# Five waits in the order model of a hybrid layer's mixing stage, set anew

## The chip, the cores and the metric

One Trainium2 chip, one core of it. The metric is the device time of one launch in microseconds (us). Times of the kernel before: 1146.1 us, the median of three runs (1145.75 to 1147.96).

## The reference

One layer on 512 tokens of width 1024, in float32: a SwiGLU half step (inner width 2816), a mixing step with two branches side by side, a second SwiGLU half step, a final norm. The mixing step is where the change is:

```python
h = rms_norm(x, mix_norm[l]); proj = h @ w_in[l]
p_rwkv, p_att, p_gate = jnp.split(proj, [RWKV_COLS, RWKV_COLS + ATT_COLS], axis=-1)
y_rwkv = rwkv7_branch(p_rwkv, ...)      # delta-rule recurrence over the tokens, 8 heads of 64
y_att = attention_branch(p_att, ...)    # window of 128, 8 query heads, 2 key heads, sinks
gate_rwkv, gate_att = jnp.split(jax.nn.sigmoid(p_gate), 2, axis=-1)
merged = gate_rwkv * (y_rwkv @ w_branch_rwkv[l]) + gate_att * (y_att @ w_branch_attn[l])
x = x + merged @ w_out[l]
```

## The kernel before, in words

Activations lie transposed, channels on the partitions and the 512 tokens along the free axis. Every large product is made of three matmuls (`mm3`, lines 216 to 218) of a rounded high half and a low half of each operand. ScalarE rounds a weight tile to its high half (line 196), VectorE subtracts it to get the low half (line 197), so each weight tile costs VectorE one pass.

The mixing stage computes 34 **jobs**, one per 128 columns of `w_in`: a job is 24 matmuls of 128 by 512. A job's result is evacuated by VectorE or, for the 16 gate jobs `g0` to `g15`, copied by ScalarE (`gt`, line 700), multiplied on GpSimd (line 701) and written to DRAM (`gd`, line 702). Later it is loaded again (line 1307 for the attention half, line 1329 for the other) and goes through a sigmoid on ScalarE (lines 1308 and 1330).

Beside this **dense** stream run five **lanes**, written as Python generators:

- `prep(i)`, one per pair of heads (i = 0 to 3), turns the columns `k`, `r`, `v` into chunked operands: `AR`, `BK` (VectorE, lines 868 to 883), then the Gram matrices `GT` (16 rows of small matmuls in two halves, line 895 on; their PSUM banks are emptied by VectorE on line 899), transposes of `BK`, and `UV`. Sums over heads go through `head_sums` (lines 802 to 813): VectorE makes a low half (line 807), then two matmuls with `bones` (lines 810 and 811).
- `solve(i)` inverts the triangular blocks on VectorE (lines 941 and 943) with DMA round trips, and ends with a load of `GI` (line 1003).
- `wkv(i)` is the recurrence: VectorE transposes `GI` into `YT` (lines 1016 and 1017), then come short rounds of small matmuls, each followed by copies on ScalarE and VectorE (lines 1027, 1037, 1038, 1057, 1058, 1069 to 1071, 1088 to 1104), six steps from chunk to chunk (line 1109), the output, and a norm through `head_sums`. `wkv(2)` and `wkv(3)` are the last ones.
- `att_kv` and `att(i)`: scores, softmax (`S`, lines 1223 to 1245), transposes of `S`, the product with the values.

When all lanes have ended come the products with `w_branch_attn` (96 matmuls on the operands `yas`) and `w_branch_rwkv` (96 matmuls on `xh`, `xl` again, whose operands are the split results of the `wkv` lanes, line 222), then `w_out`.

**What sets the order.** `interleave` (line 100) runs the generators once, before anything runs on the chip. `pe.clock` is a running sum of modelled TensorE time. A lane that yields a wait w over 300 is resumed when the clock has advanced by 1.15 w + 200 (`SLACK`, ns); one that yields less, by w. While no lane is ready, dense quarters of six matmuls (1390 ns each) are issued; a share of them is also issued beside lane work (`RATIO`, `LUMP`). So a wait decides only how much dense work stands between a lane's step and its next one in the engines' queues. The tile framework then schedules the instructions that the program gives it, and adds the semaphores. Each engine takes its queue in order. PSUM banks for small products come from two rings of three banks, "a" and "b" (`pssm`); a new product on a ring waits until the bank from three products before has been emptied.

```python
yield WSUM                                 # head_sums, line 808: 13 uses
yield 1000.0                               # prep, line 884: after AR's second half
yield 0.0                                  # prep, line 901: after GT's evictions
yield 1800.0                               # wkv, line 1018: after the transposes of GI
yield 1600.0                               # att, line 1246: after S is scaled
```

Of the kernel before, what the change touches and what calls it, by code (L numbers as in the profile page):

```python
# [50 lines left out]
LATE = 6  # L51
GEV = 1
AHEAD = 2
WSUM = 1200.0
HOP = 900.0
SLACK = 1.15, 200.0

# [74 lines left out]
def hybrid_layer_kernel(  # L132
# [47 lines left out]
    def pssm(st="a"):  # L180
        return ps.tile([P, T], F32, tag="sm" + st, name="sm", bufs=3)
# [620 lines left out]
    def head_sums(x_, sx="a"):  # L802
# [4 lines left out]
        v.tensor_tensor(out=lo, in0=x_, in1=hi.bitcast(F32), op=ALU.subtract)  # L807
        yield WSUM
        o = pssm(sx)
# [17 lines left out]
    def prep(i):  # L827
# [53 lines left out]
        yield 1200.0  # L881

        v.tensor_tensor(out=AR[:, :, 1, :], in0=c3(rm), in1=c3(E2), op=ALU.mult)
        yield 1000.0


        while i > 1 and i - 2 not in ended:
# [2 lines left out]
        for n2 in range(0, NCH // 2, 2):  # L890
            pg = [pssm().rearrange("p (n a c) -> p n a c", n=2, c=C) for h in (0, 1)]
            with sp.together():
                for n in (n2, n2 + 1):
                    for m in (0, 1):
                        for h in (1, 0):
                            sp.matmul(pg[h][:, n - n2, m:4:2, :], lhsT=BK[HS[h], 2 * n + m, :, :],
                                      rhs=AR[HS[h], 2 * n + m, :, :], start=True, stop=True)
            for h in (0, 1):
                v.tensor_tensor(out=GT[:, n2:n2 + 2, h, 0:4, :], in0=pg[h],
                                in1=gmask.unsqueeze(1).broadcast_to([P, 2, 4, C]), op=ALU.mult)  # L900
            yield 0.0
        for n2 in range(0, NCH // 2, 2):
            pt_ = pssm()
            for j in range(4):
# [102 lines left out]
    def wkv(i, sx):  # L1007
# [7 lines left out]
        YTv = YT.rearrange("p (n c) -> p n c", c=32)  # L1015
        v.transpose(YTv[0:32], GI[0:32, :, 0:32])
        v.transpose(YTv[64:96], GI[64:96, :, 0:32])
        yield 1800.0
        p1 = pssm(sx)
        with sp.together():  # L1020
            for n in range(NCH):
# [183 lines left out]
    def att(i):  # L1205
# [37 lines left out]
        v.reciprocal(out=dn, in_=dn)  # L1243
        yield 5000.0
        v.tensor_tensor(out=S, in0=S, in1=dn.unsqueeze(3).broadcast_to([P, 2, NB, P]), op=ALU.mult)
        yield 1600.0

        Pc = slot("Pc2", (P, 2, T))
        Pp = S.rearrange("p h b c -> p h (b c)")
# [30 lines left out]
    def lane_p(j):  # L1280
        for i in (j, j + 2):
            while i > 1 and st[i - 1] is None:
                yield 300.0
            yield from prep(i)
            yield from solve(i, st[i])

    def lane_w(j):
        for i in (j, j + 2):
            yield from wkv(i, "ab"[j])

    def lane_a():
        yield from att_kv()
        for i in range(4):
            yield from att(i)
        yield 3000.0
        load_yas()
        yield 3000.0
# [165 lines left out]
```

## Time and profile before

| | |
|---|---|
| median of 3 runs | 1146.1 us |
| the profiled execution | 1146.73 us |
| its span in the profile | 1145.0 us |
| granted TensorE clock, mean over the span | 0.994 |
| TensorE matmul busy | 1110.8 us, 97% |
| VectorE busy | 867.9 us, 76% |
| ScalarE busy | 588.8 us, 51% |
| GpSimd busy | 224.4 us, 20% |

The mixing stage lies at 395 to 717 us of the span. The profile's matmul ends are modelled and matmuls overlap, so the start-to-start distance of matmuls, not their length, tells TensorE's pace. Engine names in rows: PE is TensorE, PEld its weight loads, DVE VectorE, ACT ScalarE, POOL GpSimd, SP the queue of DMA issues (SPq). "[0.95 <-DVE GT L899]" behind a row means that the engine had been idle for 0.95 us and that a VectorE instruction of line 899 released it.

### The profile page before, as it was taken

The numbers are of one execution on the slowest core, as the hardware profiler recorded it, in microseconds if no ns is written. First come the engines' busy times: TensorE is split into PE (matmuls) and PEld (weight loads), VectorE is DVE, ScalarE is ACT, GpSimd is POOL, SyncE is SP. The second block draws the span as 40 slices with busy tenths as digits, with TensorE's granted clock in tenths as the row PEclk, the third lists the DMA queues.
The fourth block names the chain that finished last, engine by engine and source line by source line (L and its number), as shares of the span: only waits on it lengthen the run. The fifth ranks groups of instructions, "written<-read, shape, count | busy, mean of one in ns | idle before, by whom it ended". The sixth has DMA issues, their size and how long they took to land.

```text
span 1145.0 us, 19776 instructions
## 1 busy us (share of the span) xinstructions
PE 1110.8 (97%) x7892; PEld 963.3 (84%) x7892; DVE 867.9 (76%) x1149; ACT 588.8 (51%) x943; POOL 224.4 (20%) x164
## 2 busy tenths in 40 slices
PE   9899999999999999899989999999999999999997
PEld 7699899978997687678767877778999899989985
DVE  6978579955988479999697635778996489945865
ACT  5744145523555665557553656467554155523554
POOL 5022024402301000000111220012431034202200
PEclk9999999999999999999999999999999999999999
DMA  9234323432226453434325634933334233432221
GB/s 269 64 92 130 92 76 109 129 94 74 70 74 184 138 182 72 107 100 121 91 82 142 167 105 147 268 118 100 95 111 129 74 93 109 132 96 71 75 92 74
DMA packets 223068, 130.12 MB, mean 114 GB/s; under 512 B 37727, under 2 KB 204448, under 8 KB 222976
## 3 DMA queue, kind: packets, MB, share of 16 engines
q1 hardware_dynamic: 221248, 126.79, 38.4%
q10 hardware_dynamic: 1184, 2.04, 0.6%
q8 instruction: 62, 1.02, 0.4%
q0 software_dynamic: 544, 0.04, 0.1%
q14 instruction: 30, 0.25, 0.1%
HBM read 112.96 MB, written 15.61 MB: 112 GB/s over the span
## 4 chain that ended last, share of the span: by engine, by line
PE 72%; DVE 16%; DMA 4%; ACT 4%; issue 2%; SPq 1%; POOL 0%; ACTq 0%; DVEq 0%
PE sm L441 32%; PE mm L216 9%; PE mm L217 8%; PE mm L218 8%; PE sm L218 3%; PE sm L216 3%; PE sm L217 3%; DVE wl L197 3%; PE sm L90 3%; DVE pr L941 2%; DMA g<-gd 1%; ACT wh L196 1%; DMA wr<-in_ffn_w_gate_dram 1%; DVE xt L400 1%; DVE W L943 1%
## 5 line engine op out<-in xcount | busy, mean ns | idle before, releaser
L197 DVE TENSOR_TENSOR wl<-wr,wh 128x1024 fp32r<-128x1024 f32 (+2 forms) x149 | 208.3, 1398 | 80.8 <-ACT wh L196 80.1
L196 ACT CAST wh<-wr 128x1024 fp32r<-128x1024 f32 (+2 forms) x149 | 147.6, 990 | 219.2 <-PE mm L217 99.5
L429 POOL TENSOR_TENSOR wx<-wr,wx 128x1024 f32<-128x1024 f32 x40 | 115.2, 2881 | 386.2 <-DVE wl L197 249.8
L441 PE MATMUL sm<-th,wh 128*128 128x256 f32 x640 | 181.0, 283 | 0.9 <-DVE xt L429 0.9
L197 DVE TENSOR_TENSOR wl<-wx,wh 128x1024 fp32r<-128x1024 f32 x100 | 160.3, 1609 | 27.4 <-ACT wh L196 26.6
L441 PE MATMUL sm<-tl,wh 128*128 128x256 f32 x640 | 180.2, 282 | 0.0
L441 PE MATMUL sm<-th,wl 128*128 128x256 f32 x640 | 180.1, 281 | 0.0
L196 ACT CAST wh<-wx 128x1024 fp32r<-128x1024 f32 x100 | 104.9, 1049 | 132.2 <-PE sm L441 79.7
L441 PE MATMUL sm<-xh,wl 128*128 128x256 f32 x480 | 135.9, 283 | 0.6 <-DVE wl L197 0.6
L441 PE MATMUL sm<-xh,wh 128*128 128x256 f32 x480 | 136.0, 283 | 0.0
L441 PE MATMUL sm<-xl,wh 128*128 128x256 f32 x480 | 135.7, 283 | 0.0
L216 PE MATMUL mm<-xh,wh 128*128 128x512 f32 x320 | 131.1, 410 | 1.2 <-ACT wh L196 0.9
L218 PE MATMUL mm<-xh,wl 128*128 128x512 f32 x320 | 127.6, 399 | 3.2 <-DVE wl L197 2.9
L217 PE MATMUL mm<-xl,wh 128*128 128x512 f32 x320 | 126.5, 395 | 0.0
L441 PEld LDWEIGHTS sm<-th,wh 128*128 128x128 f32 x640 | 120.7, 189 | 2.1 <-issue 1.4
L441 PEld LDWEIGHTS sm<-tl,wh 128*128 128x128 f32 x640 | 120.6, 189 | 0.0
L441 PEld LDWEIGHTS sm<-th,wl 128*128 128x128 f32 x640 | 120.4, 188 | 0.0
L441 PEld LDWEIGHTS sm<-xh,wl 128*128 128x128 f32 x480 | 91.7, 191 | 0.8 <-DVE wl L197 0.8
L441 PEld LDWEIGHTS sm<-xh,wh 128*128 128x128 f32 x480 | 91.7, 191 | 0.5 <-ACT acc L1346 0.2
L441 PEld LDWEIGHTS sm<-xl,wh 128*128 128x128 f32 x480 | 91.7, 191 | 0.5 <-issue 0.2
L218 PEld LDWEIGHTS mm<-xh,wl 128*128 128x128 f32 x320 | 60.5, 189 | 18.4 <-DVE wl L197 3.8
L216 PEld LDWEIGHTS mm<-xh,wh 128*128 128x128 f32 x320 | 60.5, 189 | 16.1 <-issue 2.0
(391 smaller groups left out, 2259.4 us busy)
## 6 DMA issues: line engine op xcount, KB each, us to landing
wr<-in_ffn_w_down_dram SPq DMA_DIRECT2D x38, 512.0 KB, 4.1
wr<-in_w_in_dram SPq DMA_DIRECT2D x34, 512.0 KB, 4.2
wr<-in_ffn_w_gate_dram SPq DMA_DIRECT2D x42, 256.0 KB, 3.0
wr<-in_ffn_w_up_dram SPq DMA_DIRECT2D x42, 256.0 KB, 3.4
wx<-in_ffn_w_gate_dram SPq DMA_DIRECT2D x40, 256.0 KB, 3.0
wx<-in_ffn_w_up_dram SPq DMA_DIRECT2D x40, 256.0 KB, 3.5
gd<-gt SPq DMA_DIRECT2D x16, 256.0 KB, 2.3
g<-gd SPq DMA_DIRECT2D x16, 256.0 KB, 3.3
```

The lines of the kernel that those rows point to most:

```text
L90: self.keep(self.pe.matmul(out, lhsT=lhsT, rhs=rhs, **k))
L196: s.copy(out=hi[:, c], in_=raw[:, c])
L197: v.tensor_tensor(out=lo[:, c], in0=raw[:, c], in1=hi[:, c].bitcast(F32), op=ALU.subtract)
L216: pe.matmul(acc, lhsT=ah, rhs=bh, start=(first and k == 0), stop=False)
L217: pe.matmul(acc, lhsT=ah, rhs=bl, start=False, stop=False)
L218: pe.matmul(acc, lhsT=al, rhs=bh, start=False, stop=(last and k == n - 1))
L400: v.scalar_tensor_tensor(out=t_[:, 1 + i, :], in0=b0, scalar=g1, in1=b1, op0=ALU.mult, op1=ALU.add if i == 2 else ALU.subtract)
L429: e.tensor_tensor(out=o, in0=a, in1=b, op=op)
L441: pe.matmul(acc, lhsT=x_, rhs=y_, start=first and j == 0 and k == 0 and i == 0, stop=last and k == n - 1 and i == 2, skip_group_check=True)
L941: v.tensor_tensor(out=pv_[:, m], in0=a_[:, m].unsqueeze(2).broadcast_to(sh), in1=b_[:, m].rearrange("p u c -> p c u").unsqueeze(1).broadca ...
L943: v.tensor_reduce(out=o, in_=pv_, axis=AX.X, op=ALU.add)
```

## The change

Five waits of the order model get larger numbers. No instruction of the program is added or taken away, and no operand changes.

```diff
-WSUM = 1200.0
+WSUM = 1800.0
...
         v.tensor_tensor(out=AR[:, :, 1, :], in0=c3(rm), in1=c3(E2), op=ALU.mult)
-        yield 1000.0
+        yield 2400.0
...
                 v.tensor_tensor(out=GT[:, n2:n2 + 2, h, 0:4, :], in0=pg[h],
                                 in1=gmask.unsqueeze(1).broadcast_to([P, 2, 4, C]), op=ALU.mult)
-            yield 0.0
+            yield 1400.0
...
         v.transpose(YTv[64:96], GI[64:96, :, 0:32])
-        yield 1800.0
+        yield 2900.0
...
         v.tensor_tensor(out=S, in0=S, in1=dn.unsqueeze(3).broadcast_to([P, 2, NB, P]), op=ALU.mult)
-        yield 1600.0
+        yield 2800.0
```

What it moves is seen in the order of the instructions on each engine. Three places follow, each before and after. In them `mm<-xh,wh`, `mm<-xl,wh` and `mm<-xh,wl` are dense matmuls, `sm` is a small product's bank.

**First place**, TensorE, the Gram matrices of the first pair, `prep(0)`. Before:

```order
L90 MATMUL sm<-AR,BK 128x2x64 x9
L217 MATMUL mm<-xl_148,wh 128x512
L218 MATMUL mm<-xh_140,wl 128x512
L216 MATMUL mm<-xh_141,wh 128x512
L217 MATMUL mm<-xl_149,wh 128x512
L218 MATMUL mm<-xh_141,wl 128x512
L216 MATMUL mm<-xh_142,wh 128x512
L217 MATMUL mm<-xl_150,wh 128x512
L218 MATMUL mm<-xh_142,wl 128x512
L90 MATMUL sm<-AR,BK 128x2x64 x7
L96 MATMUL sm<-ident,BK 128x128 x4
```

Now, at the same place:

```order
L90 MATMUL sm<-AR,BK 128x2x64 x8
L810 MATMUL sm<-hi,bones 128x512
L811 MATMUL sm<-lo,bones 128x512
L216 MATMUL mm<-xh_141,wh 128x512
L217 MATMUL mm<-xl_149,wh 128x512
L218 MATMUL mm<-xh_141,wl 128x512
L216 MATMUL mm<-xh_142,wh 128x512
L217 MATMUL mm<-xl_150,wh 128x512
L218 MATMUL mm<-xh_142,wl 128x512
L90 MATMUL sm<-AR,BK 128x2x64 x8
```

The head sum of the other lane now stands between the two halves, and takes a bank of the same ring "a"; the transposes of `BK` have moved twelve dense matmuls further back.

**Second place**, TensorE, the start of the last recurrence, `wkv(3)`. Before:

```order
L218 MATMUL mm<-xh_142,wl 128x512
L90 MATMUL sm<-YT,GT 32x32 x16
L216 MATMUL mm<-xh_143,wh 128x512
L217 MATMUL mm<-xl_151,wh 128x512
L218 MATMUL mm<-xh_143,wl 128x512
L216 MATMUL mm<-xh_144,wh 128x512
L217 MATMUL mm<-xl_152,wh 128x512
L218 MATMUL mm<-xh_144,wl 128x512
L90 MATMUL sm<-GI,YT 32x32 x16
```

Now:

```order
L218 MATMUL mm<-xh_146,wl 128x512
L90 MATMUL sm<-YT,GT 32x32 x16
L216 MATMUL mm<-yas,wh 128x512
L217 MATMUL mm<-yas,wh 128x512
L218 MATMUL mm<-yas,wl 128x512
L216 MATMUL mm<-yas,wh 128x512
L217 MATMUL mm<-yas,wh 128x512
L90 MATMUL sm<-GI,YT 32x32 x16
```

Before, 84 dense matmuls of the jobs came after the first row of `wkv(3)`, between its rounds; now all jobs are done ahead of it. Between its rounds, up to its last output matmul, stand 26 of the 96 `yas` matmuls, where before there were 78 dense ones (six more followed).

**Third place**, ScalarE, the copies of `wkv(3)` (L1027 to L1104) and the sigmoids of the gates (L1308, L1330). Before:

```order
L1308 ACTIVATE g<-g 128x512
L1027 COPY YT<-sm 32x256 x2
L1038 COPY GI<-sm 32x8x32
L1308 ACTIVATE g<-g 128x512
L1057 COPY t<-sm 128x512
L1058 COPY t<-sm 128x448
L196 CAST wh<-wr 128x1024
L700 COPY gt<-mm 128x512
L1070 COPY UV<-sm 64x8x64
L1071 COPY AR<-sm 128x7x64
L1308 ACTIVATE g<-g 128x512
```

Now:

```order
L700 COPY gt<-mm 128x512
L1027 COPY YT<-sm 32x256 x2
L1308 ACTIVATE g<-g 128x512
L1038 COPY GI<-sm 32x8x32
L1057 COPY t<-sm 128x512
L1058 COPY t<-sm 128x448
L1308 ACTIVATE g<-g 128x512
L1070 COPY UV<-sm 64x8x64
L1071 COPY AR<-sm 128x7x64
L196 CAST wh<-wr 128x512
L1330 ACTIVATE g<-g 128x512 x2
L1104 ACTIVATE GT<-sm,qn 128x64
```

Now the copy of the last gate job, `g15`, stands right ahead of L1027, and the two L1308 are those of `g14` and `g15`; before, the sigmoids at this place were those of jobs done earlier.

## Rows read from the trace of the kernel before

**Rows 1.** The page, busy time of each engine over the whole span.

```profile
PE 1110.8 (97%) x7892; PEld 963.3 (84%) x7892; DVE 867.9 (76%) x1149; ACT 588.8 (51%) x943; POOL 224.4 (20%) x164
```

**Rows 2.** Busy time by stretches of 20 us; the first line names the columns.

```profile
core 0: us, PE busy (x) PEld busy (x) DVE busy (x) ACT busy (x) POOL busy (x), PEclk, DMA share, GB/s
460.00:480.00 20.00, 18.27 (x124) 13.75 (x124) 19.75 (x40) 7.42 (x14) 0.64 (x4) 1.00 0.39 74
...
660.00:680.00 20.00, 19.07 (x315) 15.37 (x314) 10.44 (x15) 10.52 (x19) 4.09 (x4) 1.00 0.29 94
```

**Rows 3.** TensorE's waits at 395 to 715 us: us in total, times, longest.

```profile
PE sm L90 <- DVE GT L899: 3.4, 3, 1.3
PE mm L218 <- DVE wl L197: 1.9, 1, 1.9
PE sm L90 <- DVE BK L880: 1.4, 2, 1.0
PE sm L811 <- DVE lo L807: 1.4, 3, 0.7
PE sm L96 <- DVE S L1245: 1.3, 1, 1.3
PE sm L90 <- DVE YT L1017: 1.3, 1, 1.3
...
PE sm L90 <- DVE S L1226: 0.7, 1, 0.7
PE sm L810 <- ACT hi L805: 0.6, 1, 0.6
PE sm L96 <- DVE GT L899: 0.6, 1, 0.6
PE sm L90 <- ACT YT L1027: 0.6, 1, 0.6
PE sm L90 <- ACT AR L1071: 0.3, 1, 0.3
PE sm L90 <- ACT t L1057: 0.2, 1, 0.2
```

**Rows 4.** The same columns as in rows 2, around the start of wkv(2).

```profile
618.00:620.00 2.00, 1.44 (x33) 1.31 (x34) 1.94 (x4) 0.69 (x2) 0.00 (x0) 0.94 0.94 337
620.00:622.00 2.00, 2.00 (x20) 1.16 (x21) 1.93 (x3) 0.04 (x1) 0.00 (x0) 0.50 0.01 4
622.00:624.00 2.00, 2.00 (x85) 1.87 (x80) 0.55 (x2) 0.36 (x1) 0.00 (x0) 0.70 0.17 40
```

**Rows 5.** TensorE's timeline around wkv(3): start us, us long, what.

```profile
658.13 0.39 PE L216 MATMUL mm<-xh,wh 128*128 128x512 f32 x1
...
660.62 0.39 PE L218 MATMUL mm<-xh,wl 128*128 128x512 f32 x1
660.94 0.69 PE L90 MATMUL sm<-YT,GT 32*32 32x32 f32 x32
...
717.27 0.40 PE L216 MATMUL mm<-xh,wh 128*128 128x512 f32 x1
```

**Rows 6.** The chain that ended last, 685 to 693 us: start us, us, what.

```profile
685.50 1.31 POOL gt L701
...
686.83 2.46 DMA gd<-gt
...
689.31 3.69 DMA g<-gd
```

**Rows 7.** ScalarE's timeline in wkv(3).

```profile
678.07 0.63 ACT L1308 ACTIVATE g<-g 128x512 f32<-128x512 f32 x1 [4.63 <-DMA g<-gd]
```

**Rows 8.** Waits of the SP queue at 395 to 715 us.

```profile
SPq L189 <- DVE wl L197: 69.2, 23, 7.5
```

**Rows 9.** VectorE's timeline: the first eviction of prep(0), the last split after wkv(3).

```profile
435.45 1.28 DVE L899 TENSOR_TENSOR GT<-sm,gmask 128x512 f32<-128x512 f32 x2
...
712.97 0.68 DVE L222 TENSOR_TENSOR xl<-o,xh 128x512 fp32r<-128x512 f32 x1
```

## The prediction

> **What bounds the kernel now.** I read first the page's busy times: TensorE is busy 97% of the span, the next engine 76% [rows 1]. So nearly all the time is TensorE's own work, and a change of order can win only what TensorE waits. The change adds no instruction, so TensorE's work stays, and the whole question is how long it stands still in the mixing stage. The second view, TensorE's waits in that stage, lists where: twelve kinds of waits, 13.7 us together [rows 3] (the one left out there lies ahead of the lanes). Eight of the twelve end with VectorE; the longest groups are the evictions of the Gram matrices, a weight's low half, `BK`, the low half of a head sum, the scaled `S` and the transposes of `GI`. Five of these six are the places whose waits are set anew. Of the 13.7 us, 1.8 come in and behind `wkv(3)` (0.6 for the copy of `YT`, 0.2 for `t`, 0.6 for `hi`, and one of the three for `lo`, taken as 0.4 of the 1.4); 11.9 come ahead of it. The third view, busy time by stretches, tells why: at 460 to 480 us VectorE is busy 19.75 of 20 us and TensorE waits for it, while at 660 to 680 us VectorE has 9.6 us free [rows 2].
>
> One more loss has no releaser. [...] It cost (0.06 + 0.50 + 0.30) x 2 = 1.7 us. The profiled execution took 1146.7 us, 0.6 above the median of the runs; I work against it and take the 0.6 off at the end.
>
> **What the change gives.** More dense matmuls stand between a step of VectorE and TensorE's use of it. A dense matmul takes 0.226 us (twelve begin from 658.13 to 660.62 us, 2.49 us for eleven distances) [rows 5], so 600 ns more of wait are about three of them, 1400 ns seven, before the scheduler's own shifts. That is enough for waits of 0.6 to 1.9 us each. If all the waits ahead of `wkv(3)` went, and with the one for `YT` the slow spell, 11.9 + 1.7 = 13.6 us would come back.
>
> **What stays of them.** *First place.* The second half of `prep(0)`'s Gram matrices now has a head sum ahead of it that takes a bank of the same ring of three. So it needs both evictions, where before the first was enough. The pair takes 1.28 us [rows 9], so the second comes some 0.6 us later. As many matmuls stand ahead as before. The wait of 1 us there (a third of 3.4 [rows 3]) becomes 1.8 by my estimate. *First recurrence.* The order puts the first lane's softmax, `solve(1)` and `wkv(0)` closer together on VectorE than before, so the first step of the recurrence waits for its two `AR` sums behind solve work. The trace does not show this; from below it is nothing, from above the longest single wait of a kind, 1.9 [rows 3]. I take 1.5, since VectorE is as full there as at 460 us. *Others.* The waits for a bank of `S` (0.7) and for `AR` (0.3) [rows 3] are at no place that is changed: 0.8 stays. Sum 4.1, and 13.6 - 4.1 = **9.5 us gained**.
>
> **What the end pays.** The dense work is a fixed stock, 34 jobs. What stands earlier is missing later. Before, 84 dense matmuls came behind the first row of `wkv(3)`, 19.0 us of cover for a chain of small matmuls, copies and six dependent steps. Now none does, and the 96 `yas` matmuls, which came after the chain, must do it: 26 of them, 5.9 us, inside the chain, where 78 dense ones were (17.6 us). So 11.7 us of cover go. From below, TensorE waits 1.8 us in the last part as now; from above, 1.8 + 11.7 = 13.5. I walk through the rounds, by the durations of the copies between them. The copy of `YT` stands behind a weight cast and a gate copy: 0.4 us. Before the matmuls on `t`, ScalarE has to run the sigmoid of `g14`, whose product goes through GpSimd, a write and a load, 1.31 + 2.46 + 3.69 = 7.5 us [rows 6]. That is a wait of the kind that took 4.63 us before [rows 7], but with dense matmuls beside it. Here I take 2.5 us, about half. The evictions of `UV` and `AR` run one behind the other: 1.3. The `AR` sums: 0.4. The six steps, with two or three `yas` matmuls between them in place of six: 0.2 each, 1.2. The last norm: 0.4, as now. Sum 6.2, so 4.4 us more than the 1.8 of now.
>
> Behind the chain, the norm and the splits of `wkv(3)`'s result ended at 713 us before, when TensorE came to the next products only at 717.27 [rows 5, 9]. That slack of 4 us and the 59 `yas` matmuls that stand behind the norm's own (13.3 us) cover it; I add nothing, and where they fall short the next products wait for line 222.
>
> *The clock.* In before's `wkv(3)`, with dense matmuls between the rounds, the clock stayed at 1.00 [rows 2]. With waits and small matmuls alone it fell at `wkv(2)` [rows 4]. The new end looks more like the second. I charge one more spell, 1.7 us. [...]
>
> Sum: -9.5 + 4.4 + 1.7 = **-3.4 us**: 1146.7 - 3.4 = 1143.3 by the profiled execution, 1142.7 by the median. What this measurement can tell from no change is 0.2%, 2.3 us. With the first recurrence between 0 and 1.9, the clock with or without its spell and the waits at the end between 4 and 8 us, this case's own range is 1140 to 1145.5.
>
> **The rivals.** *The end is covered.* The `yas` matmuls suffice, ScalarE does not stand, and the clock holds: 0.6 of new waits and no spell, so -9.5 + 0.6 = -8.9, 1137.2. For it: before, TensorE waits only 1.8 us there, and VectorE is half free at the end [rows 2, 3]. Against it: the two sigmoids stand inside the chain.
>
> *The waits move on.* VectorE at 460 us has 0.25 us of 20 free [rows 2]. More dense matmuls bring their own low halves and evacuations to the same queue; a wait covered here reappears at the next step that nobody set. If 8 us stay of the 13.6 in place of 4.1, -3.4 + 3.9 = +0.5, 1146.6. This is also the case that the change does not do what it says: the numbers fit the old queue, and the new order makes another one, as at the first place. Against it: the TensorE work ahead of each step grows faster than VectorE's, since a job takes 24 x 0.226 = 5.4 us of TensorE.
>
> *The end stands behind the loads.* Mechanism: SP issues in order, and between the load of `g14` and the write of `g15` stands a load of a `yas` weight, which waits for a buffer that VectorE frees. The longest such wait was 7.5 us [rows 8]. The load of `g15` is then late by as much, with it the sigmoid ahead of line 1070, and everything behind that in ScalarE's queue, which is `wkv(3)` itself. Price up to 7.5 us: -3.4 + 7.5 = +4.1, 1150.2. It makes the kernel slower by over 0.2% from a delay of 5.7 us on. For it: such waits are many there, 23 with 69 us in all. Against it: by then VectorE has little to do, so the buffer should be free. [...]
>
> **How the numbers follow.** The forecast gets 0.45, of which about 0.36 lie below 1143.8 us and 0.09 within 2.3 us of before. The covered end gets 0.18, all faster. Waits that move on get 0.16, nearly all within 0.2%. The late loads get 0.21, slower. That is 0.54 faster, 0.25 the same, 0.21 slower. The range goes from 1136, just below the covered end, to 1149.5, which leaves out the late loads at full price and little else.
>
> **What would show it.** Right: TensorE's waits for lines 899, 880, 1245 and 1017 ahead of `wkv(3)` fall from 8 us to under 3; one wait of 1.5 us or more stays at the first place; the clock holds at `wkv(2)`; TensorE reaches the products on `xh` at about 714 us in place of 717; ScalarE's line 1308 waits for its load, and TensorE waits between the rounds of `wkv(3)`. Wrong: TensorE waits under 3 us in all behind the first row of `wkv(3)` (the end is covered), or its waits ahead of it sum to 8 us or more (they moved), or a wait for a load holds line 1070 for over 5 us (the loads). A difference behind 720 us would not be explained by anything here: the order is the same there.

## The result, and the profile after

The change makes the kernel slower: 1152.25 us, the median of five runs (1150.64 to 1155.92), against 1145.75 for the kernel before in the same five rounds (1143.79 to 1147.96). The ratio is 1.0064, with a 95% interval of 1.0044 to 1.0084. The profiled execution took 1151.59 us with a span of 1149.9, so it is 0.7 below the median; its mean granted clock is 0.990 where before it was 0.994.

The page's busy times first, as [rows 1]:

```profile
PE 1115.9 (97%) x7892; PEld 970.2 (84%) x7892; DVE 875.2 (76%) x1149; ACT 588.9 (51%) x943; POOL 227.6 (20%) x164
```

The instruction counts are the same, but TensorE is busy 5.1 us longer, so the clock is the first suspect. TensorE's waits (a long one is called a hole below), as [rows 3], from 395 to 722 us (the stage ends 3 us later now):

```profile
PE sm L90 <- DVE GT L899: 3.8, 2, 3.1
PE sm L90 <- DVE AR L1102: 3.6, 2, 1.8
PE sm L90 <- DVE Pc L1254: 1.6, 1, 1.6
PE sm L90 <- ACT YT L1027: 1.4, 1, 1.4
PE sm L90 <- DVE YT L1017: 0.9, 1, 0.9
PE sm L90 <- ACT GT L1109: 0.9, 1, 0.9
PE sm L90 <- DVE YT L1016: 0.8, 1, 0.8
PE mm L218 <- DVE wl L197: 0.7, 1, 0.7
PE sm L90 <- DVE S L1226: 0.6, 1, 0.6
PE sm L90 <- ACT t L860: 0.2, 1, 0.2
```

They sum to 14.5 us; without the low half behind the first `xh` product 13.8, where before it was 13.7. So the total of the waits is the same. The waits for `BK` (1.4), for a head sum's low half (1.4) and for S (1.3) are gone, and others stand in their place. TensorE's timeline shows where the longest ones lie:

```profile
607.78 0.48 PE L90 MATMUL sm<-AR,BK 64*128 64x128 f32 x2
611.40 2.07 PE L90 MATMUL sm<-AR,BK 64*128 64x128 f32 x14 [3.13 <-DVE GT L899]
613.40 0.79 PE L216 MATMUL mm<-xh,wh 128*128 128x512 f32 x1
614.00 0.63 PE L217 MATMUL mm<-xl,wh 128*128 128x512 f32 x1
614.42 0.63 PE L218 MATMUL mm<-xh,wl 128*128 128x512 f32 x1
...
650.58 0.41 PE L90 MATMUL sm<-GT,AR 128*128 128x64 f32 x2 [1.79 <-DVE AR L1102]
...
679.26 0.69 PE L90 MATMUL sm<-YT,GT 32*32 32x32 f32 x32
...
682.72 1.45 PE L90 MATMUL sm<-GI,YT 32*32 32x32 f32 x32 [1.41 <-ACT YT L1027]
```

The first group is the second half of `prep(3)`'s Gram matrices. Behind it a dense matmul takes 0.42 us from start to start (614.00, then 614.42), where it took 0.226 before: the clock has fallen. The windows of 2 us show both spells (columns as in [rows 2]; the granted clock is the one behind the busy times); the one of the kernel before, at 618 to 624 us [rows 4], is gone:

```profile
608.00:610.00 2.00, 0.27 (x2) 0.07 (x1) 2.00 (x2) 0.00 (x0) 1.66 (x1) 1.00 0.00 0
610.00:612.00 2.00, 0.60 (x6) 0.60 (x7) 2.00 (x4) 0.00 (x0) 0.00 (x0) 0.82 0.00 0
612.00:614.00 2.00, 2.00 (x14) 1.68 (x13) 2.00 (x3) 0.00 (x0) 0.00 (x0) 0.50 0.08 12
614.00:616.00 2.00, 2.00 (x6) 1.54 (x5) 2.00 (x4) 0.00 (x0) 0.00 (x0) 0.50 0.33 100
616.00:618.00 2.00, 2.00 (x10) 1.87 (x9) 1.30 (x3) 0.00 (x0) 0.00 (x0) 0.50 0.78 201
...
682.00:684.00 2.00, 1.13 (x32) 1.02 (x32) 0.00 (x0) 1.01 (x3) 1.26 (x1) 0.74 0.65 183
684.00:686.00 2.00, 2.00 (x67) 1.82 (x62) 0.41 (x1) 0.99 (x2) 0.00 (x0) 0.50 0.64 212
686.00:688.00 2.00, 2.00 (x6) 1.16 (x4) 0.00 (x0) 1.02 (x2) 0.00 (x0) 0.50 0.02 6
688.00:690.00 2.00, 2.00 (x41) 2.00 (x42) 0.00 (x1) 0.32 (x1) 0.00 (x0) 0.55 0.94 286
```

Counted as in the prediction, each spell takes 3.4 us of full clock, 6.8 together against 1.7 before. In both, small matmuls fill part of the time, so the loss is less than that. Each begins within 0.3 us of the end of a long wait (611.3 and 683.0 us). The lower clock is not an accident of the profiled execution: all five runs of the change have a mean granted clock of 0.990 or 0.991, where the 138 runs of the kernel before that stand beside the experiments have 0.992 to 0.998, 0.9936 in the mean. Over 1150 us that is some 4 us of full clock, an estimate from these means.

Three landmarks cut the span: the first Gram product of `prep(0)`, the first `xh` product, the first `w_out` product. From the first to the second ("mix") took 285.5 us before and 289.8 now; from the second to the third ("third stage") 23.4 and 25.0; what lies behind the third 404.4 and 404.6. Ahead of the first landmark the profiled executions differ by up to 4.3 us among themselves, whatever the kernel, so the table of the experiments gives "mix" and "third" alone. Part of that difference is the clock too: at about 370 us, where no order was changed, 12 of the 19 profiles have a spell of 3.4 us at 0.50 and 7 have none.

### The profile page after: what moved, and what is told of

It is laid out like the page before. It is cut to its first block, busy times and chain, and to the rows that moved or that the text cites. A ratio compares the mean times of both kernels' runs of the same rounds, so it can differ in the third digit from the quotient of the medians.

```text
span 1149.9 us, 19783 instructions
## 1 busy us (share of the span) xinstructions
PE 1115.9 (97%) x7892; PEld 970.2 (84%) x7892; DVE 875.2 (76%) x1149; ACT 588.9 (51%) x943; POOL 227.6 (20%) x164
## 4 chain that ended last, share of the span: by engine, by line
PE 72%; DVE 16%; ACT 4%; DMA 3%; issue 3%; SPq 1%; ACTq 0%; DVEq 0%
PE sm L441 32%; PE mm L216 8%; PE mm L218 8%; PE mm L217 8%; PE sm L90 4%; PE sm L218 3%; PE sm L216 3%; PE sm L217 3%; DVE wl L197 3%; DVE pr L941 2%; ACT wh L196 1%; DMA wr<-in_ffn_w_up_dram 1%; PE sm L67 1%; DVE xt L400 1%; DVE W L943 1%
## 5 line engine op out<-in xcount | busy, mean ns | idle before, releaser
L197 DVE TENSOR_TENSOR wl<-wr,wh 128x1024 fp32r<-128x1024 f32 (+2 forms) x149 | 211.5, 1420 | 75.8 <-ACT wh L196 69.8
```

Source lines behind the costliest of these rows:

```text
L197: v.tensor_tensor(out=lo[:, c], in0=raw[:, c], in1=hi[:, c].bitcast(F32), op=ALU.subtract)
```

## The experiments

All ratios are to runs of the kernel before beside each kernel; "mix" and "third" come from the one profiled execution of each. A profile can lie up to 3.6 us from its kernel's median (e1's), so times are judged by the medians. Where the intervals of two kernels overlap, a difference between these two is not shown.

| run | median, us | ratio (95%) | mix | third |
|---|---|---|---|---|
| before (beside them) | 1144.9 to 1145.8 | 1 | 285.5 | 23.4 |
| the change | 1152.25 | 1.0064 (1.0044 to 1.0084) | 289.8 | 25.0 |
| e1 prep's waits alone | 1149.37 | 1.0039 (1.0024 to 1.0055) | 289.3 | 25.8 |
| e2 the other three alone | 1145.56 | 1.0005 (0.9994 to 1.0017) | 287.5 | 24.0 |
| e3 without YT's | 1153.63 | 1.0067 (1.0049 to 1.0084) | 292.5 | 24.4 |
| e4 without S's | 1151.52 | 1.0049 (1.0035 to 1.0064) | 288.6 | 24.2 |
| e5 change, sigmoids late | 1149.55 | 1.0040 (1.0026 to 1.0054) | 286.8 | 25.4 |
| e6 change, S late | 1152.28 | 1.0065 (1.0046 to 1.0084) | 291.3 | 26.1 |
| e7 both of these | 1149.06 | 1.0034 (1.0022 to 1.0046) | 286.4 | 25.4 |
| e8 prep's waits, sigmoids late | 1144.73 | 0.9998 (0.9989 to 1.0007) | 283.0 | 25.2 |
| e9 e5, evictions first | 1147.45 | 1.0019 (1.0008 to 1.0030) | 283.8 | 25.4 |
| e10 e8 with WSUM | 1151.07 | 1.0048 (1.0032 to 1.0064) | 285.5 | 25.6 |
| e11 e8 with S's | 1152.36 | 1.0065 (1.0049 to 1.0080) | 289.0 | 25.2 |
| e12 e9, GpSimd's sum later | 1147.43 | 1.0010 (1.0002 to 1.0019) | 287.4 | 23.6 |
| e13 e8, GpSimd's sum later | 1145.76 | 1.0006 (0.9992 to 1.0020) | 280.8 | 23.4 |
| e14 e9, the sum later still | 1143.38 | 0.9984 (0.9973 to 0.9995) | 284.6 | 23.0 |
| e15 e8, the sum later still | 1142.32 | 0.9978 (0.9964 to 0.9992) | 281.8 | 23.2 |
| e16 before, with e15's additions | 1141.92 | 0.9973 (0.9962 to 0.9984) | 285.4 | 23.6 |
| e17 e16 with the sum at its old place | 1144.14 | 0.9987 (0.9977 to 0.9996) | 286.2 | 23.3 |

**Which of the five numbers.** The prediction names two places to lose: VectorE's queue ahead of `wkv(3)`, and the end without dense matmuls of jobs. In e1 the stock ends where it ends in the change; in e2 it ends as before.

```diff
# e1: before, with these two alone (e2: the other three alone)
-        yield 1000.0
+        yield 2400.0
...
-            yield 0.0
+            yield 1400.0
```

> Of the change only the two waits of prep (2400 and 1400). All jobs still end ahead of wkv(3), as in the change, and the evictions of prep(3)'s Gram matrices still stand behind solve(2)'s last products and the scaled S of att(3). If the change's loss comes from these two things, whichever of them it is, this kernel loses most of it: 1149 to 1153 us, with a clock spell at about 611 us, another in wkv(3), or both. If it comes from the other three values, or from all five together, this one is at 1146 or below, and neither spell is there.

> The change without prep's two waits (WSUM, YT and S are set, prep is as before). 84 dense matmuls of the jobs come after the first row of wkv(3), as before the change, and S of att(3) stands behind prep(3)'s evictions. Theory 'queue' (the waits moved on in VectorE's queue, and the long hole at prep(3) costs a clock spell) and theory 'end' (the dense stock is used up) both give no loss here: 1142 to 1146.5 us, no spell in wkv(3), no wait over 2 us for line 899. If it is as slow as the change (1150 or more), both are wrong, and the new order costs by something else.

e2 costs nothing, e1 costs 3.9 us. So prep's two waits alone cost more than half of the change's 6.5 us, and the other three are harmless by themselves. In e1's trace the hole at `prep(3)` is absent (the waits for line 899 are 0.6 us in all). Its large hole lies in `wkv(3)`, and ScalarE's timeline shows what made it:

```profile
679.62 0.58 ACT L700 COPY gt<-mm 128x512 f32<-128x512 f32 x1
680.23 0.75 ACT L1027 COPY YT<-sm 32x256 f32<-32x256 f32 x2
...
683.50 0.54 ACT L1058 COPY t<-sm 128x448 f32<-128x448 f32 x1
689.36 0.63 ACT L1308 ACTIVATE g<-g 128x512 f32<-128x512 f32 x1 [5.32 <-DMA g<-gd]
690.01 0.58 ACT L1070 COPY UV<-sm 64x512 f32<-64x512 f32 x1
690.61 0.53 ACT L1071 COPY AR<-sm 128x448 f32<-128x448 f32 x1
```

TensorE, in the same run:

```profile
691.20 1.06 PE L90 MATMUL sm<-GT,AR 64*64 64x64 f32 x16 [3.29 <-ACT AR L1071]
```

That hole has 3.29 us, and a spell of 3.4 us begins with its end. (e1's profile has another spell, of 13.6 us from 496.8 us, behind a wait of 1.91 us for the first YT transpose; e8 below keeps that wait.) The sigmoid of `g15` waits 5.32 us for its load, and the recurrence's own copies of `UV` and `AR` stand behind it in the queue, though their operands had been ready. GpSimd began its product for `g15` at 680.28 and the sigmoid began at 689.36: 9.1 us for product, write and load, where the prediction had worked out 7.5 [rows 6]. No weight load held it: SP issued the write at 681.61 and the load at 685.27 with nothing between them.

**One value back.** Two more subsets, since each changes the order in another way.

> The change with one value back: YT's wait is 1800 again. The order then has S of att(3) behind the first two evictions of prep(3), not ahead of them; solve(2)'s last products stay ahead; 6 dense matmuls are left after wkv(3)'s first row. Theory 'queue': the 3.1 us hole of TensorE at prep(3) shrinks by S's 2.3 us to about 1, the spell at 611 us shrinks or goes (up to 3.4), so 1146 to 1149 us. Theory 'end': the stock is as empty as in the change, the spell in wkv(3) stays, 1150.5 to 1153 us.

> The change with one value back: S's wait is 1600 again. The order then has prep(3)'s four evictions ahead of S of att(3) by 40 rows and ahead of solve(2)'s last pair, and 24 dense matmuls (5.4 us) of jobs after wkv(3)'s first row in place of none. Theory 'queue': no hole at prep(3), no spell there, 1145 to 1148 us even though the stock is nearly empty. Theory 'end': the spell in wkv(3) stays for the most part, so 1149 to 1152 us. Theory 'any shuffle costs the same': 1150 or more with holes at other places.

Neither of the two theories fits; for e4, the third (any shuffle costs the same) does. e3 still has a hole of 3.6 us for line 899 with S out of the way, and one of 3.7 us in `wkv(3)` behind another late sigmoid. e4 has no hole at the evictions and none over 0.7 us in `wkv(3)`, and is slow all the same: 2.3 us for `BK` in `prep(3)`, 5.8 us in four waits for the YT transposes (lines 1016 and 1017). Each new order has holes of its own. So from here I took single holes away by hand and left the rest of the order as it was.

**The sigmoids.** In the change only the sigmoids of `g14` and `g15` are told to stand behind the last step of `wkv(3)`:

```diff
# e5: the change; e7: e6; e8: e1; each with
-            s.activation(at(1, n + 1), pz[:, n, :], AF.Copy, scale=q[:, n:n + 1])
+            copied.append(s.activation(at(1, n + 1), pz[:, n, :], AF.Copy, scale=q[:, n:n + 1]))
...
-        s.activation(m2, m2, AF.Sigmoid)
+        with tc.issue_after(copied[-1].ins) if k >= 6 else nullcontext(): s.activation(m2, m2, AF.Sigmoid)
# e6, e7: the change, with
-        yield 5000.0
+        yield 5000.0 if i < 3 else 7000.0
         v.tensor_tensor(out=S, in0=S, ...
```

> The change, with the sigmoids of the last two gate jobs (line 1308 for g14 and g15) put behind wkv(3)'s last step in ScalarE's queue; nothing ahead of wkv(3) moves. Theory 'loads' (in wkv(3) ScalarE stands still for gate loads, TensorE waits for the copies behind them, and the clock falls): the two waits of line 1308 for g (1.1 and 2.5 us) leave the recurrence, and TensorE reaches the first xh product 1 to 3 us earlier, so 1149 to 1151 us. The 1.4 us wait for the YT copy stays, since the copy of g15 ahead of it waits for a write and is not moved. Theory 'prep(3)' (the 3.1 us hole at 608 us and the spell behind it are the loss): no change, 1151.5 to 1153 us.

> The change, with one wait of att(3) made longer (7000 in place of 5000 ahead of the scaling of S). Up to prep(3) the order is the same; there S stands behind the first two evictions, no solve row stands between wkv(2)'s two AR sums any more, and the products on S come later. Theory 'prep(3)': S is 2.3 us of VectorE's time, so the hole of 3.1 us falls to 0.8 to 1.5, the spell at 611 us goes or shrinks, and the wait of 1.8 us at 650 us goes, so 1146 to 1149.5 us. Theory 'loads': 1151 to 1153 us, unchanged.

> Both of the last two edits in one. If they act on separate losses, their gains add: 1144.5 to 1148 us, no spell at 611 us and no wait for a load of g inside wkv(3). If the loss has a third source (the third stage behind 720 us, or any new order of this kind), it stays at 1149 us or more.

> Prep's two waits alone, with the sigmoids of g14 and g15 behind wkv(3)'s last step. With prep's waits alone the sigmoid ahead of line 1070 waited 5.3 us for its load and TensorE 3.3 us for line 1071, with a spell of 2.7 us behind it. Theory 'loads': that hole and its spell go, 3 to 5 us less than prep's waits alone (1149.4), so 1144.5 to 1147 us. Theory 'the hole moves': the chain of copies or the wait for the YT copy stands there in its place, 1148 to 1150 us.

The medians fall by 2.7 us in the change (1152.25 to 1149.55), by 3.2 with S late (1152.28 to 1149.06), and by 4.6 with prep's waits alone (1149.37 to 1144.73), where that is the whole loss. Only for the last do the two intervals not meet; the change's and e5's overlap. Two of the three are shown in place: from `wkv(3)`'s first product to the first `xh` product it takes 41.5 us in e1 (679.22 to 720.70) and 37.0 in e8 (676.71 to 713.68), 41.6 in e6 and 36.7 in e7, and the waits for line 1071 of 3.3 and 3.5 us are gone; in e8 TensorE waits 0.5 us in all from 660 to 712 us. For the change itself it is not: this stretch has 41.0 us in its profile and 41.1 in e5's, where the wait for `YT` (1.5 us) and the spell behind it stay, since the copy of `g15` ahead of it waits for a write and was not moved. What e5's profile gains lies ahead of `wkv(3)`, where the order is the same. So e5's 2.7 us are a median without a place, and the clock does not tell it either: it is 0.989 to 0.991 in all six runs.

S late brought nothing, and its trace says why. VectorE's queue at `prep(3)`, first in the change, with GpSimd's row beside it, then in e6:

```profile
607.51 1.03 DVE L941 TENSOR_TENSOR pr<-W,Y 128x512 f32<-128x512 f32 x1
608.45 2.29 DVE L1245 TENSOR_TENSOR S<-S,sm 128x1024 f32<-128x1024 f32 x1
610.67 1.27 DVE L899 TENSOR_TENSOR GT<-sm,gmask 128x512 f32<-128x512 f32 x2
```

```profile
607.91 1.75 POOL L701 TENSOR_TENSOR gt<-gt,rs 128x512 f32<-128x512 f32 x1 [3.90 <-ACT gt L700]
```

```profile
606.17 1.04 DVE L941 TENSOR_TENSOR pr<-W,Y 128x512 f32<-128x512 f32 x1
607.11 2.31 DVE L197 TENSOR_TENSOR wl<-wr,wh 128x1024 fp32r<-128x1024 f32 x1
609.34 1.28 DVE L899 TENSOR_TENSOR GT<-sm,gmask 128x512 f32<-128x512 f32 x2
611.13 1.21 DVE L1245 TENSOR_TENSOR S<-S,sm 128x1024 f32<-128x1024 f32 x1
```

A weight's low half took S's place and took as long: 2.31 us, where a row of that form takes 1.21 at 612.46 us in the change. S, out of that place, takes 1.21. It is the place that is slow (GpSimd works beside it, in e6 from 606.54 to 608.34 us, see the last section), and the hole stayed at 3.17 us.

**The evictions first.**

```diff
# e9: e5, with prep's evictions kept in a list, and for solve(2)'s second product and S of att(3)
-                bmm(o[:, 0, r:r + 2], ...
+                with tc.issue_after(evicted[-1].ins) if i == 2 and a_ is W else nullcontext(): bmm(...
...
-        v.tensor_tensor(out=S, in0=S, ...
+        with tc.issue_after(evicted[-1].ins) if i == 3 else nullcontext(): v.tensor_tensor(out=S, ...
```

> The change with the sigmoids of g14 and g15 behind wkv(3)'s last step (1149.55 us), and in addition VectorE's second product of solve(2) and S of att(3) put behind the first two evictions of prep(3)'s Gram matrices. TensorE's order is the same but for a few rows. S alone behind them had left the hole of 3.2 us, since a weight's low half took its place and solve(2)'s rows stayed ahead. Theory 'VectorE's queue at prep(3)': the evictions now come some 3 us earlier, the hole is 0 to 1 us, the spell at 611 us goes, 1145 to 1147 us. Theory 'it moves on': the same VectorE work has to be done before prep(3) and wkv(2) go on, so the wait reappears at the second evictions, the YT transposes or the AR sums of wkv(2), 1148.5 to 1150 us.

2.1 us less than e5, 1147.45, between the two expectations; the two intervals just overlap. In the profile the hole and the spell at 611 us are gone, but 2.1 us of waits came back at the second evictions:

```profile
615.87 0.65 PE L96 MATMUL sm<-ident,BK 128*128 128x128 f32 x4 [1.22 <-DVE GT L899]
617.41 1.15 PE L90 MATMUL sm<-cen,g 64*64 64x64 f32 x32 [0.89 <-DVE GT L899]
```

"Mix" falls by 3.0 us all the same, although TensorE stands idle as long as in e5 (11.6 and 11.7 us): what went is clock, one spell and half of the one in `wkv(3)`. Over e9's twelve runs the granted clock is 0.988 to 0.996, 0.993 in the mean, against 0.990 for e5.

**Which value on top of prep's.**

> Prep's two waits and WSUM, with the two sigmoids behind wkv(3)'s last step; YT and S as before the change. It asks which of the three values that cost nothing by themselves costs 4.8 us on top of prep's waits (1144.7 with prep's waits alone, 1149.5 with all five, both with the sigmoids moved). If WSUM does: 1148 to 1150 us, with a hole at the first recurrence (wkv(0)'s first step) or at prep(3). If not: 1144 to 1146 us.

> Prep's two waits and S, with the two sigmoids behind wkv(3)'s last step; WSUM and YT as before the change. If S's wait costs on top of prep's: 1148 to 1150 us. If WSUM does: 1144 to 1146 us here. If it needs both, or any further value brings its own new holes, this one and the one with WSUM lie in between, 1146 to 1148 us.

Both are as slow as all five with the sigmoids moved (e5) or slower. Their profiles have one long hole in common, 3.2 us for the first YT transpose, and others that differ: 1.8 us each at a head sum and an `AR` sum in e10, 2.8 for the copy of `AR` in `wkv(2)` in e11. (e10's profile is the fastest of its six runs and shows little of the loss.) The question was wrong: by the medians the losses are no property of a value, and they don't add.

**The third stage.** With both repairs 2 us are left between the first `xh` and the first `w_out` product. VectorE and GpSimd there, in the change:

```profile
733.04 0.68 DVE L197 TENSOR_TENSOR wl<-wr,wh 128x512 fp32r<-128x512 f32 x1
734.62 2.84 DVE L222 TENSOR_TENSOR mg<-g,mg 128x512 fp32r<-128x512 f32 x1 [0.90 <-ACT mg L221]
737.38 0.68 DVE L1335 TENSOR_TENSOR g<-g 128x512 f32<-128x512 f32 x1
```

```profile
734.51 2.40 POOL L429 TENSOR_TENSOR wx<-wx 128x1024 f32<-128x1024 f32 x1 [38.88 <-DMA g<-gd]
```

and in the kernel before:

```profile
724.65 0.69 DVE L1335 TENSOR_TENSOR g<-g 128x512 f32<-128x512 f32 x1
727.46 0.69 DVE L1334 TENSOR_TENSOR g<-g,mm 128x512 f32<-128x512 f32 x1 [2.12 <-ACT g L1330]
```

```profile
725.58 2.40 POOL L429 TENSOR_TENSOR wx<-wx 128x1024 f32<-128x1024 f32 x1 [29.58 <-PE mm L217]
```

Before, GpSimd's sum fell for the most part into 2.1 us in which VectorE waited. Now the low half at 734.62 stands beside it and takes 2.84 us, where the next one, at 739.18, takes 0.68, and the rows behind it in VectorE's queue come later by 2.2 us, among them line 1334, which empties the bank that a later product needs. TensorE then waits 1.0 us at 738.8; in e5, with the same meeting, 1.6 us, and for line 1334.

```diff
# e12: e9, e13: e8, with a copy on GpSimd that waits for the last merged tile, and the sum behind it
             mg.append((h_, l_))
+        behind = g.tensor_copy(out=behind_t, in_=m1[:, 0:1])
...
-        hh = ffn_h(ffn2_w_gate[0], ...
+        with tc.issue_after(behind.ins) if hi_ == 0 else nullcontext(): hh = ffn_h(ffn2_w_gate[0], ...
# e14, e15, e16: the copy reads the low half of that tile instead
+        behind = g.tensor_copy(out=behind_t, in_=l_[:, 0:1].bitcast(F32))
```

> The change with both repairs (sigmoids of g14 and g15 behind wkv(3), solve(2)'s second product and S behind prep(3)'s evictions: 1147.45 us), and GpSimd's first sum of two weight tiles for the last half step (line 429, 2.4 us) held behind the last merged tile. With the change that sum runs at 734.5 us, and the VectorE row beside it takes 2.84 us in place of 0.68; before the change it ran at 725.6 us, where VectorE stood idle for 2.1 us. Theory 'GpSimd beside VectorE': the stretch from the first xh product to the first w_out product, 25.4 us, falls to 23.5 to 24, so 1145 to 1146.3 us. Theory 'the stage's loads are late' (it is longer since its weights and gates are loaded later): it stays at 25 us or more, 1147 to 1148 us. A collision may come back behind 745 us, where VectorE has more time.

> Prep's two waits alone, with the sigmoids behind wkv(3)'s last step (1144.73 us, no different from before), and the same hold on GpSimd's sum, which there ran at 728.1 us beside a VectorE row of 2.89 us. Ahead of 680 us TensorE waits some 5 us less than before the change in that kernel. Theory 'GpSimd beside VectorE': 1 to 1.5 us less, 1143 to 1144 us, below both kernels. Otherwise 1144.5 to 1145.5 us.

> As e12_gpsimd_later, but GpSimd's sum is held behind the low half of the last merged tile, not behind the tile itself. In e12 the stretch from the first xh to the first w_out product fell from 25.4 to 23.6 us as expected, but the sum then ran beside that low half (2.85 in place of 0.68 us), and TensorE waited 1.9 us for it. Behind it VectorE has nothing to do for some 2.5 us. Theory 'GpSimd beside VectorE': both waits are gone, 1145 to 1146 us, no VectorE row of a merged tile over 1.3 us. Theory 'it moves on again': a weight's low half of w_out is hit, TensorE waits 1 us or more there, 1147 to 1148 us.

> As e13_prep_best, with the same later hold. The stretch behind the first xh product had 23.0 us there, and a wait of 1.8 us for the low half of the last merged tile right behind it. If that wait goes: 1142.5 to 1144.3 us, faster than both kernels. If it comes back at the next row: 1144.5 to 1146 us.

In e12 the third stage fell from 25.4 to 23.6 us, as it should by a collision, and the collision came back at the last low half, behind the third landmark, with the total unchanged:

```profile
747.21 2.85 DVE L222 TENSOR_TENSOR mg<-g,mg 128x512 fp32r<-128x512 f32 x1 [0.69 <-ACT mg L221]
```

TensorE waited 1.9 us for it. e13 went the same way: its third stage fell from 25.2 to 23.4 us, TensorE waited 1.8 us for the last low half, and 1145.76 us shows no gain over e8. In e14 and e15 the sum meets one short row alone that no product waits for (`xt`, 1.6 us in place of 0.4), both waits are gone, and both kernels are faster than before the change. That looked like the gain the prediction had promised, so the kernel before got the same additions:

> The kernel before the change with the same two additions as e15_prep_last (the sigmoids of g14 and g15 and GpSimd's sum held back); its five waits are the old ones. In the kernel before, those two sigmoids stand behind wkv(3) anyway, and GpSimd's sum runs at 725.6 us, while VectorE stands idle. Theory 'GpSimd beside VectorE': nothing to win here, 1144.8 to 1146 us, and the gain of e15_prep_last (1142.3) belongs to prep's waits. If it is at 1143 us or below, the later sum is a gain by itself, and prep's waits have won nothing.

> As e16_before_gpsimd (1141.9 us), but GpSimd's sum is not held: the small tile and the copy into it are there, and the sum stands ahead of the copy, as in the kernel before. If e16's gain of 3 us comes from the later sum (and the loads that move with it on SP's queue), this kernel is at 1144.5 to 1146 us. If it comes from the small tile (which shifts the other tiles' addresses) or from chance in the first stage, where e16's profile had 2.4 of its 3 us, it is at 1141.5 to 1143 us.

e16 is the fastest of all, 1141.92 us, by 0.27% (0.16 to 0.38) below the kernel before, with the old five waits. Its "mix" and "third" are those of before; what its profile shows of the gain lies ahead of the first Gram product (2.4 us) and behind the third stage (0.7). e17, with the tile and the copy but the sum at its old place, took 1144.14 us, a ratio of 0.9987 (0.9977 to 0.9996). By the medians about half of the 3 us comes with the added tile or copy, and the rest with the later sum and the weight loads that move with it on SP's queue; but the intervals of e16 and e17 overlap, so the second half is not shown. Why either helps is not settled. The profiles put most of it ahead of the first Gram product, where nothing was moved: 427.9 to 430.7 us in the six kernels with the tile, 429.1 to 432.3 in the others. The ranges overlap, and the spell at 370 us takes part in them (ten of the thirteen profiles without the tile have it, two of the six with it), so this points to the tile and shows nothing. Measured on the same footing, the five new waits with both repairs (e14) stand at 1143.38, prep's alone (e15) at 1142.32, and the old waits (e16) at 1141.92. So of the change's 6.5 us some 1.5 are left, and the intervals of e14 and e16 overlap; the edges of e9 stand in e14 alone, and what they would do to the old waits was not run. The new numbers win nothing that these runs can show, even when everything they are known to break is mended. The granted clocks hint at why: 0.992 in the mean of e15's twelve runs, 0.994 in e16's, some 2 us of full clock. What prep's waits save in waits may be what the clock takes back; that is an estimate and not shown.

## Why the prediction was wrong, step by step

*"What bounds the kernel"* held: the stage is TensorE's work, its waits and its clock, and nothing else of the change showed ahead of 717 us.

*"What the change gives", 13.6 us, and "What stays of them", 4.1.* This is the step that failed first. Ahead of `wkv(3)` TensorE waits 12.2 us in the change where it waited 11.8 (the sum of the waits in the timeline, in the change from 0.21 at 434 us to 0.86 at 654). The five covered waits did shrink: lines 899, 880, 1245 and 1017 together from 8 to 4.7 us, without the hole at `prep(3)` to 1.5 (0.63 and 0.87). But I counted what would be covered and listed only the waits that stayed at their old places. I did not look for new ones along VectorE's queue, where at `prep(3)` 5.8 us, mostly of `solve(2)` and S, had come to stand ahead of the evictions (from 604.9 us, when the first half's matmuls ended, to 610.67). The first place, taken as 1.8 us, cost 0.8 (0.21 and 0.63); the first recurrence's `AR` sums, taken as 1.5, cost 1.77. The rival "the waits move on" was right in kind, and its own sign (8 us or more ahead of `wkv(3)`) came true. Its price was not: it let 8 us stay, and 12.2 stayed.

That prep's waits do cover something is shown by e8: up to 680 us TensorE stands idle 7.7 us where it was 12.8 before (sums over the windows of 2 us). In its profile part of that was paid back in the third stage (1.8 us) and by a spell twice as long as before's; the medians are the same.

*"What the end pays", 6.2 us of waits.* Over-sized: behind `wkv(3)`'s first row TensorE waited 1.4 us in the profiled execution, one wait for the copy of `YT`, where I had 0.4 for it. By the sign I had set (under 3 us) the end was covered. (The slack behind the chain, read as 4 us, was 3.6, since the last split ended at 713.65; nothing hung on it.) But the mechanism behind my largest term there, a sigmoid that waits for its round trip through DRAM ahead of the recurrence's copies, was real: it cost 3.2 us by e6 and e7 and 4.6 us by e1 and e8. In the profile of the change itself it is 1.1 and 2.5 us of ScalarE's waits and no wait of TensorE's, whose granted clock was 0.50 from 683.0 to 689.8 us, so that the few matmuls there filled the time; e5's 2.7 us could not be placed. The rival "the end stands behind the loads" had the place right and the cause half right. It wanted a weight load on SP's queue to make the load late; the round trip alone, 9.1 us in e1, was enough. I gave it a fifth of the chance, and its time, 1150.2 us, is the nearest of those I had named, though the change itself shows other losses too.

*"The clock", one spell of 1.7 us.* This term was too small: there were two, of 3.4 each by the same count, and the runs' mean clocks (0.990 or 0.991 in all five) say that the loss recurs. The spell at `wkv(2)` went, as forecast; the one in `wkv(3)` came, as forecast, and was twice as long; the one behind the hole at 608 us was not in the sum at all, since that hole wasn't. That an end with waits and small matmuls brings a spell was my estimate from one place, whose granted clocks give the 1.7 us [rows 4], and no run shows a rule for it: behind waits of 1.9 us in the same place e8 has a spell of 6.8 us and e15 none (last section).

*"A difference behind 720 us would not be explained by anything here."* There was one, 1.7 us. The premise was wrong: TensorE and GpSimd have the same order there, but the rows of VectorE and ScalarE and the loads on SP's queue stand in another order up to the first `w_out` products (VectorE's rows agree only from 733.3 us on before, and from 739.2 now). And engines with the same rows can still meet at other times: GpSimd's sum met another VectorE row.

The sum was -9.5 + 4.4 + 1.7 = -3.4. By the profiles it is +0.4 (waits ahead of `wkv(3)`) - 0.4 (waits behind it) + 5.1 (clock, an upper bound) for a stage that grew by 4.4 us, and +1.7 behind it; ahead of the first Gram product, where nothing was moved, the change's profile is 1.4 us shorter. So the waits came out even, and what made the stage longer is the clock, which fell to 0.50 as the two long waits ended (at 611.3 and 683.0 us). The profiled executions are 4.9 us apart and the medians 6.5; the difference has no place.

## What to carry to other kernels

When more work is put between a producer and its consumer, walk along the producer's own queue in the new order and price what now stands ahead of each result; the waits that are listed in the old profile do not tell where the new ones will be, nor how long a single one gets. On an engine that takes its queue in order, as ScalarE did in e1 (the copies of `UV` and `AR` stood behind a sigmoid that waited 5.32 us for its load), an instruction that waits for a round trip through DRAM should stand behind everything of a dependent chain, and saying so explicitly (one edge) is surer than tuning the numbers that happen to place it (e8). A version that beats the old kernel is to be compared with the old kernel that has the same repairs: here no gain of the change was left.

## What the runs showed of the hardware

Three VectorE rows shown above, with their operands in SBUF, began while a GpSimd instruction ran, and each ended behind it. The row at 734.62, 0.68 us by itself, ended at 737.46, 0.55 us behind GpSimd's sum (734.51 to 736.91); S at 608.45 took 2.29 in place of 1.21 beside a GpSimd product of 1.75 us that began at 607.91, and ended 1.08 us behind it; e6's low half at 607.11 took 2.31 in place of 1.21 beside a product that ran until 608.34. They lost 2.16, 1.08 and 1.10 us, where 2.29, 1.21 and 1.23 us of the GpSimd instruction were left: nearly all of that rest, and not a share of their speed. Line 1334, which reads a PSUM bank, was not held: in the kernel before it took its usual 0.69 us at 727.46 while GpSimd's sum ran until 727.98.

Behind the same wait one execution has a clock spell and another none. e8 and e15 have the same order up to the third stage, and both wait 1.9 us for the first YT transpose of `wkv(0)`. e8 has a spell from 495.4 to 502.2 us behind it, e15 none (nor has e13; e1's lasts 13.6 us). The windows behind that wait, of e8 and then of e15:

```profile
494.00:496.00 2.00, 0.90 (x8) 0.86 (x10) 2.00 (x6) 0.00 (x0) 0.00 (x0) 0.85 0.99 255
496.00:498.00 2.00, 2.00 (x25) 0.91 (x25) 1.94 (x9) 1.06 (x4) 0.00 (x0) 0.50 0.47 138
498.00:500.00 2.00, 2.00 (x23) 1.24 (x17) 0.56 (x4) 0.73 (x2) 0.16 (x1) 0.50 0.37 55
```

```profile
492.00:494.00 2.00, 0.85 (x10) 0.66 (x10) 2.00 (x6) 0.00 (x0) 0.00 (x0) 1.00 0.99 261
494.00:496.00 2.00, 1.43 (x36) 0.91 (x33) 1.94 (x9) 0.99 (x5) 0.00 (x0) 1.00 0.43 127
496.00:498.00 2.00, 2.00 (x75) 1.55 (x79) 1.00 (x5) 0.75 (x3) 0.09 (x1) 1.00 0.47 67
```

So a single spell in one profile may be a draw, and is not by itself a property of the order. (e15 has the added tile and e8 has not; but the change and e5, neither of which has it and whose order is the same up to `wkv(3)`, differ as well, with no spell and one of 3.4 us behind the same waits at 498 to 500 us.) That fits the scatter of e1, twelve runs from 1145.3 to 1155.2 us with mean clocks from 0.996 to 0.986, against 1143.4 to 1147.0 us for the kernel before beside it, and it is why the "mix" of a single profile should not be read finer than some 2 us. In other orders the loss is steady, as the runs of the change and of e5 show (0.989 to 0.991 in all eleven), so a spell is to be judged by the clocks of several runs.
